# A ConvFFN in seven block products for eight: the whole down projection and five pairs of up tiles of one layer

## The chip, the cores and the metric

The kernel runs on one core of one Trainium2 chip. The metric is the device time of one execution, in microseconds (us). Before the change it is 1056.19 us, the median of three runs that lie between 1055.73 and 1057.11 us. The engines are named as the profile names them: PE (TensorE, the matrix engine; PEld is its weight load), DVE (VectorE), ACT (ScalarE), POOL (GpSimd) and SP (SyncE, which issues the transfers).

## The reference, cut to what matters

Two layers of an encoder work on 512 positions of 1024 channels, in float32. Each layer mixes the positions (a Fourier group and windowed attention, not touched here) and then runs a convolutional feed-forward block, the ConvFFN:

```python
def dwconv_centred(h, w, bias):
    hp = jnp.pad(h, ((0, 0), (1, 1), (0, 0)))
    return hp[:, :-2] * w[0] + hp[:, 1:-1] * w[1] + hp[:, 2:] * w[2] + bias

    # per layer l, with D_FF = 2816
        h = rmsnorm(x, norm2[l])
        up = dwconv_centred(h @ w_up[l], conv_w[l], conv_b[l])
        gate, val = up[..., :D_FF], up[..., D_FF:]
        x = x + (jax.nn.silu(gate) * val) @ w_down[l]
```

`w_up` has 1024 rows and 5632 columns, `w_down` 2816 rows and 1024 columns.

## The kernel before, in words

**Tiles.** Everything is kept transposed: a tile holds 128 channels on the partitions and the 512 positions along the free axis. `x[k]` (k = 0 to 7) is the residual, `h2[k]` the normed input of the ConvFFN. The columns of `w_up` are 44 row tiles of 128 channels here, 22 of the gate half and 22 of the value half; tile `fi` of the one is paired with tile `fi` of the other. I call such a pair a slot.

**Precision.** Every float32 operand of a matrix product is split into a high and a low part (`split`, `wsplit`): ACT copies the high part out (line 90), DVE subtracts it from the source for the low part (line 93). `mm3` then issues three matmuls for a product of two such operands: high by high (line 120), weight low by high (line 121), weight high by low (line 122). A weight tile of 512 columns therefore costs one ACT and one DVE instruction, `whi` and `wlo`, with five buffers each.

**The up projection (lines 705 to 730).** For each of the two tiles of a slot, 24 matmuls of 128x512 gather one product in one of six PSUM banks. DVE multiplies it with the row of reciprocal norms `rb2` into `u`; ACT makes `y = cw1*u + cb`; two `scalar_tensor_tensor` on DVE (`stt`, line 96) add the two neighbours. Then ACT takes the silu of the gate tile and the product of gate and value tile follows (line 728): on DVE in layer 0, on POOL in layer 1. The result is split again.

**The down projection (lines 740 to 758).** The 22 slots are done in two halves of eleven; after each half its eleven tiles are multiplied with `w_down`: for each of eight output tiles m, 33 matmuls of 128x512 into one bank, and DVE adds the bank to `x[m]`. In the last half the last m is done in two halves of 256 columns.

**What sets the order.** The program is recorded under a tile scheduler with a simulated timeline: it decides, when the program is built, in which order each engine's instructions stand. On the chip each engine then runs its own list in that order, and waits where an operand or a buffer is not there. Just ahead of the ConvFFN stands the second norm (`norm_tile`, then `col_rstd` with the matmuls of line 227, then `row_rstd` with those of line 234), which gives `rb2`; the products of the first slots need `h2` but not `rb2`, and so can stand among its instructions.

## Time and profile before

| what | value |
|---|---|
| median of three runs | 1056.19 us |
| the profiled execution, its own time | 1056.14 us |
| span of its trace | 1054.3 us |
| PE busy | 1038.2 us, 98% |
| DVE busy | 726.8 us, 69% |
| ACT busy | 507.9 us, 48% |
| POOL busy | 90.8 us, 9% |
| layer 1's ConvFFN | from about 716 us to the end at 1054.3 us |

The span is the time from the first to the last instruction of the trace; the profiled execution's own time is 1.84 us longer. A line of the trace is that of a helper where a helper issues the instruction: line 93 is every `tt` (tensor_tensor), line 96 every `stt`, line 90 every activation. So one goes by the names of the tiles: `tF<-ps,rb` is a product times `rb2`, `wlo<-wraw,whi` the low part of a weight, `x<-x,ps` the addition to the residual. A matmul's record is longer than its turn on PE, since matmuls are pipelined; what counts is the distance between the starts of two that follow each other.

### The profile page before, as it was taken

How to read it: one execution, taken by the hardware profiler on the slowest of the kernel's cores; microseconds unless marked ns; L12 is line 12 of the kernel's file. 1: busy time of each engine (PE TensorE's matmuls, PEld its weight loads, DVE VectorE, ACT ScalarE, POOL GpSimd, SP SyncE). 2: the span in 40 equal slices, each digit the busy share in tenths (PEclk: the TensorE clock that was granted, in tenths of full speed). 3: DMA queues.
4: the chain of work that ended last, by engine and by line, in shares of the span. 5: the costliest groups of instructions: out<-in, count | busy, mean ns of one | idle time of the engine just before them, and what ended most of it. 6: DMA issues, size and time to landing. Idle time of an engine off the chain costs nothing.

```text
span 1054.3 us, 14425 instructions
## 1 busy us (share of the span) xinstructions
PE 1038.2 (98%) x5107; PEld 873.2 (83%) x5107; DVE 726.8 (69%) x1384; ACT 507.9 (48%) x939; POOL 90.8 (9%) x164
## 2 busy tenths in 40 slices
PE   8998999999999999999999999999999999999998
PEld 8986778888888888888899887888888888888887
DVE  8878768697767777777519775478877336878632
ACT  5339755455444445455423785246554224454421
POOL 0004410000000000000000152001101000101100
PEclk9999999999999999999999999999999999999999
DMA  7232152332269833239856313333332333332241
GB/s 273 83 115 87 58 193 81 100 100 96 78 226 353 324 100 101 89 114 322 280 181 221 113 62 99 122 100 94 101 101 74 96 115 100 98 101 82 82 150 48
DMA packets 60475, 140.03 MB, mean 133 GB/s; under 512 B 6642, under 2 KB 22258, under 8 KB 60404
## 3 DMA queue, kind: packets, MB, share of 16 engines
q1 hardware_dynamic: 60404, 139.12, 40.5%
q8 instruction: 40, 0.66, 0.3%
q14 instruction: 31, 0.25, 0.1%
HBM read 116.02 MB, written 23.07 MB: 132 GB/s over the span
## 4 chain that ended last, share of the span: by engine, by line
PE 93%; DVE 2%; DMA 2%; ACT 1%; issue 1%; POOL 0%; SPq 0%; ACTq 0%; DVEq 0%; POOLq 0%
PE ps L122 28%; PE ps L120 28%; PE ps L121 28%; PE ps L118 3%; PE ps L548 2%; PE ps L541 2%; PE ps L529 1%; DMA wraw<-in_w_qkv_dram 1%; PE ps L234 1%; PE ps L227 1%; ACT tA L90 0%; DMA x<-in_xT_dram 0%; DVE tA L533 0%; ACT act L90 0%; PE ps L500 0%
## 5 line engine op out<-in xcount | busy, mean ns | idle before, releaser
L90 ACT ACTIVATE whi<-wraw 128x512 fp32r<-128x512 f32 (+1 forms) x296 | 182.0, 616 | 290.8 <-PE ps L122 278.4
L120 PE MATMUL ps<-act,whi 128*128 128x512 f32 x768 | 298.9, 390 | 0.0
L121 PE MATMUL ps<-act,wlo 128*128 128x512 f32 x768 | 298.3, 389 | 0.0
L122 PE MATMUL ps<-act,whi 128*128 128x512 f32 x768 | 298.2, 389 | 0.0
L93 DVE TENSOR_TENSOR wlo<-wraw,whi 128x512 fp32r<-128x512 f32 (+1 forms) x304 | 219.7, 726 | 103.4 <-ACT whi L90 102.0
L122 PEld LDWEIGHTS ps<-act,whi 128*128 128x128 f32 x768 | 144.2, 188 | 30.1
L120 PEld LDWEIGHTS ps<-act,whi 128*128 128x128 f32 x768 | 144.2, 188 | 29.7
L121 PEld LDWEIGHTS ps<-act,wlo 128*128 128x128 f32 x768 | 144.2, 188 | 29.7
L96 DVE SCALAR_TENSOR_TENSOR tF<-tF,pb,tF 128x511 f32<-128x511 f32 x176 | 133.5, 763 | 11.1 <-ACT tF L90 8.7
L93 DVE TENSOR_TENSOR tF<-ps,rb 128x512 f32<-128x512 f32 x104 | 71.2, 689 | 77.9 <-PE ps L122 64.7
L120 PE MATMUL ps<-slab,whi 128*128 128x512 f32 (+2 forms) x212 | 82.2, 388 | 0.0
L122 PE MATMUL ps<-slab,whi 128*128 128x512 f32 (+2 forms) x212 | 79.9, 380 | 0.4 <-DVE slab L93 0.3
L121 PE MATMUL ps<-slab,wlo 128*128 128x512 f32 (+2 forms) x212 | 80.0, 378 | 0.0
L90 ACT ACTIVATE tF<-tF,pb 128x512 f32<-128x512 f32 x88 | 71.7, 816 | 11.3 <-DVE tF L93 4.6
L93 DVE TENSOR_TENSOR x<-x,ps 128x512 f32<-128x512 f32 (+1 forms) x49 | 32.9, 674 | 36.5 <-PE ps L122 36.3
L93 POOL TENSOR_TENSOR tF<-tF,tF 128x512 f32<-128x512 f32 x22 | 30.2, 1371 | 256.1 <-DVE tF L96 224.1
L120 PE MATMUL ps<-pT,whi 128*128 128x512 f32 (+1 forms) x132 | 50.5, 383 | 0.0
L121 PE MATMUL ps<-pT,wlo 128*128 128x512 f32 (+1 forms) x132 | 50.5, 383 | 0.0
L122 PE MATMUL ps<-pT,whi 128*128 128x512 f32 (+1 forms) x132 | 50.5, 383 | 0.0
L538 POOL TENSOR_SCALAR tA<-tA,den 128x256 f32<-128x256 f32 (+1 forms) x64 | 37.4, 590 | 145.1 <-DVE den L537 144.6
L533 DVE CUSTOM_DVE_ANT_0 tA<-ps,pb,nsink 128x256 f32<-128x256 f32 (+1 forms) x64 | 37.8, 603 | 14.5 <-PE ps L529 9.7
L122 PEld LDWEIGHTS ps<-slab,whi 128*128 128x128 f32 x212 | 39.7, 188 | 8.3 <-DVE slab L93 0.9
(178 smaller groups left out, 1485.0 us busy)
## 6 DMA issues: line engine op xcount, KB each, us to landing
wraw<-in_w_up_dram SPq DMA_DIRECT2D x88, 512.0 KB, 3.5
wraw<-in_w_down_dram SPq DMA_DIRECT2D x32, 512.0 KB, 3.7
kept<-tA SPq DMA_DIRECT2D x56, 256.0 KB, 5.7
whi<-kept SPq DMA_DIRECT2D x28, 256.0 KB, 3.0
wlo<-kept SPq DMA_DIRECT2D x28, 256.0 KB, 3.0
kept<-tA SPq DMA_DIRECT2D x32, 192.0 KB, 4.4
wraw<-in_w_down_dram SPq DMA_DIRECT2D x32, 192.0 KB, 2.4
wraw<-in_w_o_dram SPq DMA_DIRECT2D x8, 512.0 KB, 3.7
```

Source lines behind the costliest of these rows:

```text
L90: return nc.scalar.activation(out, in_, func, **kw)
L93: return (eng or nc.vector).tensor_tensor(out, a, b, op=op)
L96: return nc.vector.scalar_tensor_tensor(out=out, in0=a, scalar=s, in1=b, op0=op0, op1=op1)
L118: nc.tensor.matmul(out, a[0], b[0], start=start, stop=stop, **kw)
L120: nc.tensor.matmul(out, a[0], b[0], start=start, stop=False, **kw)
L121: nc.tensor.matmul(out, a[1], b[0], start=False, stop=False, **kw)
L122: nc.tensor.matmul(out, a[0], b[1], start=False, stop=stop, **kw)
L227: nc.tensor.matmul(pt[:, 2 * b:2 * b + 2], acc[:, b * P:(b + 1) * P], ones2, start=True, stop=True)
L533: nc.vector.tensor_tensor_reduce(out=pr[:, :n], in0=sc[:, :n], in1=mask[:, m0:m0 + n], scale=qs_scale[p][:, i, e:e + 1], scalar=nsink[:, l ...
L538: nc.gpsimd.tensor_scalar(pr[:, :n], pr[:, :n], den[:, i:i + 1], 1.0, op0=ALU.mult, op1=ALU.mult)
L541: tr = nc.tensor.transpose(pp[:, j * P:(j + 1) * P], pr[:, j * P:(j + 1) * P], ident)
L548: pv = nc.tensor.matmul(py[64 * e:64 * e + 64, i0 * P:(i1 + 1) * P], vp[:, j, 64 * g:64 * g + 64], pT[:, half, e, b0:b0 + 2 * (i1 - i0) + ...
```

## The change

Layer 0 is unchanged. Layer 1's ConvFFN becomes a function of its own, `conv_ffn_seven`. It uses the Winograd form of Strassen's product: two 2x2 block matrices are multiplied with seven block products for eight, and with sums of blocks instead. In the form used here the blocks of the weight give four sums s1 to s4, those of the moving operand four sums T1 to T4, and the positions are cut in two halves of 256 columns.

- **Slots.** The 22 slots are done in three groups of 6, 8 and 8 (`GROUPS`), each followed by its part of the down projection. All eight PSUM banks are used in turn (`BANKS8`), the two "tp" banks too, which `col_rstd` and `row_rstd` also use.
- **Up.** In 17 of the slots `up_eight` does what was done before. In slots 4, 8, 11, 16 and 19 (`SEVEN`) `up_seven` makes both tiles of the pair together: 84 matmuls of 128x256 in three banks X, Y and Z, in place of 48 of 128x512. It sums weights on DVE (four of 512 columns), splits seven weight blocks for four, and puts the two `u` together from the banks.
- **Sums of h2.** `seven_h` makes T1 to T4 of `h2` in the first four slots, into buffers that earlier parts of the program have left.
- **Gate.** The product of gate and value tile is a `tt` on DVE, no longer on POOL.
- **Sums of the gated tiles.** `seven_gu` takes two gated tiles, makes T1 to T4 of them and splits all seven blocks.
- **Down.** For each pair of output rows seven products, each of kp k-tiles (3 in the first group, 4 in the others) by three matmuls of 128x256, and after each an addition of 256 columns to `x` on DVE. For the first three pairs of rows the sum s1 is made by the transfers: a load issued by SP and a second one issued by POOL that adds to it (`accum_op`). The other sums are DVE's.

The helpers move down by four lines: `tt` is line 97 in the changed kernel, `stt` line 100, `act` line 94, `mm3` lines 124 to 126, `col_rstd` and `row_rstd` lines 231 and 238.

```diff
+GROUPS = [(0, 6), (6, 8), (14, 8)]
+SEVEN = (4, 8, 11, 16, 19)
+BANKS8 = ("mm", "mm", "mm", "av", "sc", "sc", "tp", "tp")
...
+    def sums_of_b(b1, b2):
+        t13, t24 = temp(512, "tF"), temp(512, "tF")
+        tt(t13[:, LO], b1[:, HI], b1[:, LO], ALU.subtract)
+        tt(t13[:, HI], b2[:, HI], b1[:, HI], ALU.subtract)
+        tt(t24[:, LO], t13[:, LO], b2[:, HI], ALU.subtract)
+        tt(t24[:, HI], t24[:, LO], b2[:, LO], ALU.add)
+        return t13, t24
+
+    def parts(g, src, keys, room):
+        two = [next(room), next(room)]
+        split(*two, src)
...
+    def seven_h(k, l, h2, room):
+        b = [temp(512, "tF") for _ in range(2)]
+        for i in range(2):
+            act(b[i], x[k + 4 * i], scale=g2[:, l, k + 4 * i:k + 4 * i + 1])
...
+        t13, t24 = sums_of_b(*b)
+        parts(g, t13, ("T1", "T3"), room)
+        parts(g, t24, ("T2", "T4"), room)
+        return g
+
+    def seven_gu(b1, b2, room):
+        t13, t24 = sums_of_b(b1, b2)
+        one = next(room)
+        g = dict(B11=[one[:, LO], one[:, HI]])
+        split(*g["B11"], b1[:, LO])
+        parts(g, b2, ("B21", "B22"), room)
+        parts(g, t13, ("T1", "T3"), room)
+        parts(g, t24, ("T2", "T4"), room)
+        return g
...
+    def up_seven(l, fi, h2, ts, rb2):
+        a, b = [wload(t["w_up"][l, fi + z * FT], 1024) for z in range(2)]
+        a11, a12, a21, a22 = a[:, :512], a[:, 512:], b[:, :512], b[:, 512:]
+        X, Y, Z = [third()[:, LO] for _ in range(3)]
...
+        product(X, wsplit(a11), "B11", True)
+        act(ua[:, LO], X)
+        s1, s2, s3, s4 = [temp(512, "tA") for _ in range(4)]
+        tt(s1, a21, a22, ALU.add)
+        product(Y, wsplit(s1), "T1", True)
+        act(ub[:, HI], Y)
+        product(Z, wsplit(a12), "B21", True)
+        tt(ua[:, LO], ua[:, LO], Z, ALU.add)
+        tt(s3, a11, a21, ALU.subtract)
+        tt(s2, s3, a22, ALU.subtract)
+        product(X, wsplit(s2), "T2")
...
+        product(X, wsplit(a22), "T4")
+        tt(ub[:, LO], X, rb2[:, LO], ALU.mult)
+        tt(ub[:, HI], ub[:, HI], rb2[:, HI], ALU.mult)
+        yield ub
...
+    def first_two(l, mp, f0, kp):
+        n = kp * P
+        s1 = temp(n, "tA")
+        nc.sync.dma_start(s1, wd(l, 2 * mp + 1, f0, kp, 0))
+        nc.gpsimd.dma_start(s1, wd(l, 2 * mp + 1, f0, kp, 1), accum_op=ALU.add)
...
+    def conv_ffn_seven(l, h2, rb2):
+        room, ts = h_rooms(), []
+        for f0, nf in GROUPS:
+            kp = nf // 2
...
+                us = (up_seven if f0 + n in SEVEN else up_eight)(l, fi, h2, ts, rb2)
...
+                if len(ts) < 4:
+                    ts.append(seven_h(len(ts), l, h2, room))
+                gate(ys)
...
+                else:
+                    gu.append(seven_gu(upper, ys[0], groom))
...
+            for mp in range(3):
+                products(mp, first_two(l, mp, f0, kp) if mp else ready)
+            for mp in range(KT // 2):
+                products(mp, other_five(l, mp, f0, kp, mp == 3))
...
+        if l == L - 1:
+            conv_ffn_seven(l, h2, rb2)
+            break
```

Three places show how this moves instructions.

**PE, at the second norm of layer 1.** The products `ps_1576`, `ps_1584`, `ps_1593` and `ps_1601` are the first four of the up projection before the change, `ps_1575`, `ps_1607` and `ps_1583` those after it; `acc` is the sum of squares of the norm. Before:

```order
L122 MATMUL ps_1576_7036<-act_1563_7003,whi_1574_7032 128x512
L122 MATMUL ps_1584_7077<-act_1563_7003,whi_1582_7073 128x512
L122 MATMUL ps_1593_7123<-act_1559_6981,whi_1591_7119 128x512
L120 MATMUL ps_1593_7123<-act_1563_7003,whi_1591_7119 128x512
L121 MATMUL ps_1593_7123<-act_1563_7003,wlo_1592_7120 128x512
L122 MATMUL ps_1593_7123<-act_1563_7003,whi_1591_7119 128x512
L121 MATMUL ps_1601_7164<-act_1527_6847,wlo_1598_7157 128x512
L122 MATMUL ps_1601_7164<-act_1527_6847,whi_1597_7156 128x512
L227 MATMUL ps_1565_7009<-ones2_118,acc_1517_6802 128x2 x4
```

After:

```order
L124 MATMUL ps_1561_6987<-act_1486_6636,whi_1555_6961 128x512
L125 MATMUL ps_1561_6987<-act_1486_6636,wlo_1556_6962 128x512
L126 MATMUL ps_1561_6987<-act_1486_6636,whi_1555_6961 128x512
L124 MATMUL ps_1575_7035<-act_1524_6827,whi_1571_7027 128x512
L125 MATMUL ps_1575_7035<-act_1524_6827,wlo_1572_7028 128x512
...
L125 MATMUL ps_1575_7035<-act_1563_7003,wlo_1574_7032 128x512
L126 MATMUL ps_1575_7035<-act_1563_7003,whi_1573_7031 128x512
L231 MATMUL ps_1565_7009<-ones2_118,acc_1517_6802 128x2 x4
L124 MATMUL ps_1607_7178<-act_1524_6827,whi_1603_7170 128x512
```

Between the last product of the mixer's output (`ps_1561`) and the matmuls of `col_rstd` there stood 78 matmuls of four up products; now there stand the 24 of one.

**DVE, among the up slots.** Before, in the middle of a half (`tF<-ps` is `u`):

```order
L93 TENSOR_TENSOR wlo_1939_8954<-wraw_1937_8951,whi_1938_8953 128x512
L96 SCALAR_TENSOR_TENSOR tF_1920_8861<-tF_1919_8859,pb_96,tF_1920_8861 128x511 x2
L93 TENSOR_TENSOR wlo_1941_8958<-wraw_1937_8951,whi_1940_8957 128x512
L93 TENSOR_TENSOR tF_1927_8900<-ps_1926_8875,rb_1569_7023 128x512
L93 TENSOR_TENSOR wlo_1948_9000<-wraw_1946_8997,whi_1947_8999 128x512
L96 SCALAR_TENSOR_TENSOR tF_1928_8902<-tF_1927_8900,pb_96,tF_1928_8902 128x511 x2
```

After, around the fourth slot (`tF_1654<-tF_1654,tF_1662` is the gate, `tF_1665`, `tF_1666` and `sq` belong to `seven_h`, `tF_1671`, `tF_1672` and `pT` to `seven_gu`):

```order
L97 TENSOR_TENSOR tF_1654_7385<-tF_1654_7385,tF_1662_7426 128x512
L97 TENSOR_TENSOR tF_1666_7435<-tF_1665_7434,tF_1664_7431 128x256
L97 TENSOR_TENSOR tF_1671_7450<-tF_1631_7284 128x256
L97 TENSOR_TENSOR tF_1671_7450<-tF_1654_7385,tF_1631_7284 128x256
L97 TENSOR_TENSOR sq_1668_7441<-tF_1665_7434,room_1667_7440 128x512
L97 TENSOR_TENSOR tF_1666_7435<-tF_1666_7435,tF_1664_7431 128x256
L97 TENSOR_TENSOR pT_1673_7458<-tF_1654_7385,pT_1673_7458 128x512
L97 TENSOR_TENSOR tF_1672_7451<-tF_1671_7450,tF_1654_7385 128x256
L97 TENSOR_TENSOR pT_1673_7458<-tF_1671_7450,pT_1673_7458 128x512
L97 TENSOR_TENSOR tF_1680_7473<-tF_1680_7473,ps_1679_7472 128x256
L97 TENSOR_TENSOR room_1670_7445<-tF_1666_7435,sq_1669_7444 128x512
```

Weight splits stood between every two of the other instructions; now eleven instructions in a row split no weight.

**DVE, where a group of slots ends and its down projection begins.** Before, in the down projection of the second half:

```order
L93 TENSOR_TENSOR wlo_2069_9659<-wraw_2067_9656,whi_2068_9658 128x512
L93 TENSOR_TENSOR x4_78<-x4_78,ps_2057_9568 128x512
L93 TENSOR_TENSOR wlo_2071_9663<-wraw_2067_9656,whi_2070_9662 128x512
L93 TENSOR_TENSOR wlo_2074_9669<-wraw_2072_9666,whi_2073_9668 128x384
L93 TENSOR_TENSOR wlo_2078_9711<-wraw_2076_9708,whi_2077_9710 128x512
L93 TENSOR_TENSOR x5_79<-x5_79,ps_2066_9620 128x512
```

After, at the end of the first group (`tF_1709<-tF_1709,tF_1723` is the last gate, `m4` a split T block of the last pair of gated tiles):

```order
L97 TENSOR_TENSOR x0_74<-x0_74,ps_1728_7728 128x256
L97 TENSOR_TENSOR x2_76<-x2_76,ps_1733_7757 128x256
L97 TENSOR_TENSOR x4_78<-x4_78,ps_1741_7792 128x256
L97 TENSOR_TENSOR tF_1709_7651<-tF_1709_7651,tF_1723_7706 128x512
L97 TENSOR_TENSOR wlo_1743_7804<-tA_1737_7783,whi_1742_7803 128x384
L97 TENSOR_TENSOR wlo_1751_7830<-tA_1747_7824,whi_1750_7829 128x384
L97 TENSOR_TENSOR wlo_1753_7844<-wraw_1746_7819,whi_1752_7843 128x384
L97 TENSOR_TENSOR tF_1724_7712<-tF_1709_7651,tF_1698_7586 128x256
L97 TENSOR_TENSOR tF_1725_7713<-tF_1724_7712,tF_1709_7651 128x256
L97 TENSOR_TENSOR tA_1765_7909<-wraw_1762_7902,tA_1763_7907 128x384
L97 TENSOR_TENSOR pT_1674_7463<-tF_1709_7651,pT_1674_7463 128x512
L97 TENSOR_TENSOR tA_1780_7991<-wraw_1777_7984 128x384
```

One addition to `x` came per output tile, with four weight splits; now additions of 256 columns, weight sums, the gate and the sums of the last gated pair stand together.

More of the change, by code (lines that the diff above doesn't have):

```diff
@@ new lines, in parts, with h_rooms @@
+    def parts(g, src, keys, room):
+        two = [next(room), next(room)]
+        split(*two, src)
+        for key, cols in zip(keys, (LO, HI)):
+            g[key] = [z[:, cols] for z in two]
+    def h_rooms():
+        for tag in ("th0", "th1", "tl0", "tl1", "wt0", "wt1", "v", "accA", "accF"):
+            yield cp.tile([P, 512], F32R, tag=tag, name=nm("room"), bufs=1)
+        z = sp.tile([P, 1024], F32R, tag="ropetab", name=nm("room"), bufs=1)
+        yield from (z[:, :512], z[:, 512:])
+        for _ in range(2):
+            yield tp.tile([P, 516], F32R, tag="tail", name=nm("room"), bufs=2)[:, :512]
+        for _ in range(2):
+            yield temp(512, "sq", F32R)
+        yield cp.tile([P, 512], F32R, tag="room", name=nm("room"), bufs=1)
@@ new lines, in seven_gu, with up_eight @@
+    def seven_gu(b1, b2, room):
[7 more added lines that the diff above has]
+        return g
+    def up_eight(l, fi, h2, ts, rb2):
+        for z in range(2):
+            w = wchunks(t["w_up"][l, fi + z * FT], 1024)
+            o = third()
+            for k in range(KT):
+                mm3(o, [q[:, (k % 4) * P:(k % 4 + 1) * P] for q in w[k // 4]], [h2[k][:, s, :] for s in range(2)],
+                    k == 0, k == KT - 1)
+            u = temp(512, "tF")
+            tt(u, o, rb2, ALU.mult)
+            yield u
@@ new lines, in conv, with gate, wd @@
+    def conv(l, m, u):
+        y = temp(512, "tF")
+        act(y, u, AF.Identity, scale=cw[:, l, 1, m:m + 1], bias=cb[:, l, m:m + 1])
+        stt(y[:, 1:], u[:, :-1], cw[:, l, 0, m:m + 1], y[:, 1:], ALU.mult, ALU.add)
+        stt(y[:, :-1], u[:, 1:], cw[:, l, 2, m:m + 1], y[:, :-1], ALU.mult, ALU.add)
+        return y
+    def gate(ys):
+        act(ys[0], ys[0], AF.Silu)
+        tt(ys[0], ys[0], ys[1], ALU.mult)
+    def wd(l, m, f0, kp, half):
+        return t["w_down"][l, m, :, (f0 + half * kp) * P:(f0 + (half + 1) * kp) * P]
@@ new lines, in other_five @@
+    def other_five(l, mp, f0, kp, first):
+        n = kp * P
+        left, right = wtile(), wtile()
+        for i in range(2):
+            nc.sync.dma_start(left[:, i * n:(i + 1) * n], wd(l, 2 * mp + i, f0, kp, 0))
+        for i in (1, 0):
+            nc.sync.dma_start(right[:, i * n:(i + 1) * n], wd(l, 2 * mp + i, f0, kp, 1))
+        a11, a21, a12, a22 = left[:, :n], left[:, n:2 * n], right[:, :n], right[:, n:2 * n]
+        if first:
+            yield "X", wsplit(a11), "B11", 0, 0, False
+            s1 = temp(n, "tA")
+            tt(s1, a21, a22, ALU.add)
+            yield "Y", wsplit(s1), "T1", 1, 1, False
+        s2, s3, s4 = [temp(n, "tA") for _ in range(3)]
+        tt(s3, a11, a21, ALU.subtract)
+        tt(s2, s3, a22, ALU.subtract)
+        yield "X", wsplit(s2), "T2", 0, 1, False
+        yield "Z", wsplit(a12), "B21", 0, 0, True
+        yield "X", wsplit(s3), "T3", 1, 1, True
+        tt(s4, a12, s2, ALU.add)
+        yield "Y", wsplit(s4), "B22", 0, 1, True
+        yield "X", wsplit(a22), "T4", 1, 0, True
```

59 lines of the change are left out of this document (56 added, 3 removed).

## The prediction

> **What bounds the kernel now.** I read the page's shares first, then the chain of waits, then the busy time by stage.
>
> ```profile
> span 1054.3 us, 14425 instructions
> PE 1038.2 (98%) x5107; PEld 873.2 (83%) x5107; DVE 726.8 (69%) x1384; ACT 507.9 (48%) x939; POOL 90.8 (9%) x164
> PE 93%; DVE 2%; DMA 2%; ACT 1%; issue 1%; POOL 0%; SPq 0%; ACTq 0%; DVEq 0%; POOLq 0%
> ```
>
> PE carries 93% of the chain, so the count of its columns sets the time, as long as nothing else holds it. Four stretches of layer 1's ConvFFN (columns: window, length, then busy time and instruction count of PE, PEld, DVE, ACT, POOL; clock; DMA share; GB/s) show how far the others are from that:
>
> ```profile
> 718.00:880.00 162.00, 162.00 (x716) 134.15 (x715) 106.91 (x147) 69.85 (x108) 15.58 (x11) 1.00 0.31 98
> 880.00:943.00 63.00, 63.00 (x279) 52.18 (x278) 49.43 (x63) 31.44 (x47) 7.73 (x6) 1.00 0.30 93
> 943.00:1000.00 57.00, 57.00 (x253) 47.19 (x252) 41.85 (x56) 26.37 (x40) 6.85 (x5) 1.00 0.30 94
> 1000.00:1054.00 54.00, 51.06 (x257) 43.45 (x255) 16.38 (x26) 10.12 (x17) 0.00 (x0) 0.99 0.31 97
> ```
>
> PE has no idle time before the tail and runs at clock 1.00; DVE is busy 66% of the first stretch and 78% of the second. This is the room into which the change puts its sums.
>
> **Prices.** PE's are the distances of starts, at 512 columns and in the last product, which is done at 256:
>
> ```profile
> 721.57 0.39 PE L121 MATMUL ps<-act,wlo 128*128 128x512 f32 x1
> 721.80 0.39 PE L122 MATMUL ps<-act,whi 128*128 128x512 f32 x1
> 722.02 0.39 PE L120 MATMUL ps<-act,whi 128*128 128x512 f32 x1
> 722.25 0.39 PE L121 MATMUL ps<-act,wlo 128*128 128x512 f32 x1
> ...
> 1049.46 0.28 PE L120 MATMUL ps<-pT,whi 128*128 128x256 f32 x1
> ...
> 1050.66 0.28 PE L121 MATMUL ps<-m,wlo 128*128 128x256 f32 x1
> 1050.78 0.28 PE L122 MATMUL ps<-m,whi 128*128 128x256 f32 x1
> ```
>
> 0.68/3 = 0.227 us and 1.32/11 = 0.120 us: a matmul of half the columns costs 53%, not 50%. DVE's prices, the same way:
>
> ```profile
> 717.00 0.68 DVE L93 TENSOR_TENSOR wlo<-wraw,whi 128x512 fp32r<-128x512 f32 x1
> 717.60 0.68 DVE L93 TENSOR_TENSOR tF<-ps,rb 128x512 f32<-128x512 f32 x1
> 718.20 3.39 DVE L96 SCALAR_TENSOR_TENSOR tF<-tF,pb,tF 128x511 f32<-128x511 f32 x5
> 721.50 0.69 DVE L93 TENSOR_TENSOR wlo<-wraw,whi 128x512 fp32r<-128x512 f32 x1
> ...
> 303.85 1.03 DVE L93 TENSOR_TENSOR tA<-m,tA 128x384 fp32r<-128x384 f32 x2 [2.09 <-ACT tA L90]
> 305.27 0.56 DVE L93 TENSOR_TENSOR tA<-m,tA 128x384 fp32r<-128x384 f32 x1 [0.40 <-ACT tA L90]
> ...
> 575.27 0.75 DVE L93 TENSOR_TENSOR act<-pT,ropetab 128x256 f32<-128x256 f32 x2
> 575.94 0.68 DVE L93 TENSOR_TENSOR slab<-tF,slab 128x512 fp32r<-128x512 f32 x1
> ```
>
> A tt of 512 columns takes 0.60 us (717.00 to 717.60), an stt 3.30/5 = 0.66, a tt of 384 columns 1.03 - 0.56 = 0.47, one of 256 columns 0.67/2 = 0.335. Here too a half costs more than half.
>
> **What PE saves.** Down: before 8 x 2 products, of which the last is halved: 495 matmuls at 0.2267 and 66 at 0.120, 120.1 us. After: 22 slots make 11 pairs of k tiles, by four pairs of rows 44 blocks of 21 matmuls at 0.120: 110.9 us. That is 9.3 us less. Up: a slot costs 48 x 0.2267 = 10.88 us, by `up_seven` 84 x 0.120 = 10.08; five of them save 4.0 us. Together **-13.3 us**. Seven for eight would be 12.5%; the dearer half columns leave 7.6%.
>
> **What DVE gets.** By these prices a slot of `up_eight` takes four wlo (2.40), two u (1.20), four stt (2.64) and now the gate (0.60), 6.85 us, beside 10.88 us of PE; half of a `seven_gu` (5 x 0.335 + 3 x 0.60 = 3.48 for two slots) makes it 8.6. A slot of `up_seven` takes seven wlo and four sums of 512 columns (6.6), the u parts (2.3), the neighbours (2.64), the gate and half a `seven_gu`: 13.9 us beside 10.08 of PE. In the first four slots each `seven_h` adds 4 x 0.335 + 2 x 0.60 = 2.54. A pair of rows of the down projection takes 8.4 us beside 10.08 (four k tiles) or 7.05 beside 7.56 (three). Over the whole ConvFFN that is 322 us of DVE beside 346 of PE, 93%; by the same prices it is 187 before.
>
> The gate costs DVE something already when it runs on POOL:
>
> ```profile
> 727.18 0.74 DVE L96 SCALAR_TENSOR_TENSOR tF<-tF,pb,tF 128x511 f32<-128x511 f32 x1
> 728.06 1.30 POOL L93 TENSOR_TENSOR tF<-tF,tF 128x512 f32<-128x512 f32 x1 [4.42 <-DVE tF L96]
> 728.44 1.47 DVE L96 SCALAR_TENSOR_TENSOR tF<-tF,pb,tF 128x511 f32<-128x511 f32 x1
> ```
>
> A DVE instruction beside it is held 0.73 us longer than its like, so the move itself is worth 0.1 us a slot to DVE. It is the sums that load it.
>
> **Where DVE makes PE wait.** An average of 93% would do if the work came evenly. It doesn't, and DVE runs its list in order. So I take, from the order of the changed program, each stretch that begins where DVE waits for a product of PE and ends where PE waits for DVE's result, count what stands between on both engines, and price it. Where DVE's sum is longer, PE stands still for the difference.
>
> 1. The second norm. In the trace before, DVE runs without a gap into the last `acc`:
>
> ```profile
> 699.13 0.75 DVE L96 SCALAR_TENSOR_TENSOR act<-x,pa,act 128x512 fp32r<-128x512 f32 x1
> 701.45 0.69 DVE L93 TENSOR_TENSOR acc<-acc,sq 128x512 f32<-128x512 f32 x1
> 707.24 0.95 PE L227 MATMUL ps<-ones,acc 128*128 128x2 f32 x8
> 689.60:707.20 17.60, 17.60 (x79) 14.60 (x78) 12.87 (x22) 7.95 (x14) 0.00 (x0) 1.00 0.32 89
> ```
>
> The 78 up matmuls between the mixer's last product and L227 kept PE busy for 17.6 us. The 24 that now stand there are 5.4 us, to about 695; the last `acc` is due at 702.1 less the two wlo that have left DVE's list, 700.9. That gives 6; by counts (25 tt and 8 stt, 20.3 us, beside 16.3 of PE) 4. I take **5**. None of it was there before: L227 came 5 us after `acc`.
> 2. The first `up_seven`. From the second up product's u to the last split of `seven_h`, which T2 and T4 wait for: 39 tt and 14 stt, 23 tt of 256 columns, 40.4 us; PE has 132 matmuls of 512 and 35 of 256, 34.1. **6.8**, with 0.5 for the wlo behind it.
> 3. The first group's end. From the T4 product of slot 4 to the first addition to `x[0]`: 7 tt of 512, 11 of 384, 14 of 256 and 6 stt, 18.0 us; PE 11 matmuls of 512 and 75 of 256, 11.5. **6.5**. Behind the late addition stand those of `x[2]` and `x[4]`, whose banks the next products need.
> 4. The second group's end. From slot 11's T4: 31 tt of 512, 18 of 256 and 10 stt, 31.3 us; PE 61 and 99 matmuls, 25.7. **5.6**, and 1.2 at slot 11 itself.
> 5. The third group's end, in the same way from slot 19: 30.7 beside 25.5, **5.2**, and 1.2.
>
> Sum: 5 + 6.8 + 6.5 + 6.8 + 6.4 = 31.5 us. In each, PE's later instructions wait behind the one that waits. By the same count the ConvFFN before has no such stretch, as the 63.00 of 63.00 us of PE show.
>
> **What else is added.** ACT gets 104 instructions, on an engine at 43 to 50% of the stretches above: nothing. The nine accumulating transfers are of a kind that this trace lacks. The nearest row:
>
> ```profile
> wraw<-in_w_down_dram SPq DMA_DIRECT2D x32, 512.0 KB, 3.7
> ```
>
> Below, nothing, as the loads are issued ahead of the stall; above, one such time in each group, 3 x 3.7 = 11 us. I take nothing, since POOL, rid of 22 gates, has little else to issue between. [...] The weight is reloaded for each matmul as before:
>
> ```profile
> L122 PEld LDWEIGHTS ps<-act,whi 128*128 128x128 f32 x768 | 144.2, 188 | 30.1
> ```
>
> A load takes 188 ns by its record, more than the 120 ns between the half matmuls of the tail, which each have one of their own; so there it is overlapped.
>
> The tail stays:
>
> ```profile
> 1051.09 0.42 DVE L93 TENSOR_TENSOR x<-x,ps 128x256 f32<-128x256 f32 x1 [3.53 <-PE ps L122]
> 1051.54 0.33 SPq L758 DMA_DIRECT2D out_dram<-x  x1
> ```
>
> The last addition and transfer are of 256 columns before and after.
>
> **The sum.** 1054.3 - 13.3 + 31.5 = 1072.5 us of span; with the 1.84 us that lie around the span of the profiled execution (1056.14, against a median of 1056.19) **1074 us**.
>
> **Rivals.**
>
> - *DVE's work is absorbed.* DVE has 7% less than PE on average, and PE stays the bound: 1056.1 - 13.3 = 1043 us. For it speaks the average; against it that instructions run in order, and that the surplus lies in five places with no slack behind. It decides by DVE's price: the five stretches hold some 141 us of DVE work, so at 12.6% less, 0.525 us for 512 columns instead of 0.60, stalls fall by 17.8 us to 13.7, about the gain. No row shows a tt of 512 columns below 0.60. 10%.
> - *Half the stalls.* Part of what I count as one after the other is hidden, by banks or by DVE having run ahead: 1056.1 - 13.3 + 16 = 1059 us. The order allows little of it. 8%.
> - *The accumulating transfers come late.* s1 is the second operand that each pair of rows needs; if its two transfers in series are not there, each group stands one landing more: 1074 + 11 = 1085 us. The loads before are ahead of need, which speaks against it. 7%.
> - *Weight loads show behind short matmuls.* If a load of 188 ns could not overlap, the 1344 half matmuls (924 down, 420 up) would each take 0.188 us more: +253 us, 1327 us. The tail's 0.120 us speaks against it, as those 66 matmuls would have needed 0.308 each. 2%. [...]
> - *The change does not do what it says.* If the scheduler had kept eight products, the time would stay at 1056; but the order shows 1344 matmuls of 128x256, so 1%.
>
> **Chances and range.** The forecast keeps 72%; within it the five stalls may be off by a quarter, 8 us, so 1066 to 1082. The range takes in the bounds of the entry and of the transfers and reaches to the half case: 1058 to 1085. Outside lie the first rival, the weight loads and tails of some 5%. What a measurement of this kernel can tell from no change is about 0.2%, 2 us. Faster holds the first rival and a little of the second, 12%; the same 3%, between them; slower 85%.
>
> **What would show it.** In the profile after: PE's busy time down to about 1025 us with 0.120 us between half matmuls everywhere, and 95 to 96% of the span; DVE's busy time up by 135, to about 860 us, with DVE as releaser of PE's idle time. PE idle in five places of 4 to 7 us: ahead of `col_rstd`, in the first `up_seven` at its T products, and at the start of each of the three down projections, there behind `x`, `wlo` and `m4` of DVE. DVE without a gap over each of these. POOL without the x22 group. Wrong would be: no gaps and a shorter span (the first rival), gaps released by a DMA on `tA` (the third), or half matmuls further apart than 0.120 us (the fourth). If the gaps are there but shorter, my prices of DVE are too high.

## The result and the profile after

The changed kernel takes **1097.22 us** (median of four runs, 1096.44 to 1098.41), the kernel before 1056.09 us in the same comparison: ratio **1.0389, 95% interval 1.0371 to 1.0407**. It is slower by 3.9%, where 1.7% was forecast; the time lies above the range's upper end of 1085 us.

From the page of the changed kernel, the span, the shares, the granted clock in 40 slices and the chain of waits by engine:

```profile
span 1095.1 us, 16049 instructions
PE 1052.7 (96%) x5650; PEld 904.3 (83%) x5650; DVE 835.6 (76%) x1693; ACT 556.8 (51%) x1043; POOL 69.6 (6%) x151
PEclk9999999999999999999999999898899998999989
PE 82%; DVE 10%; ACT 3%; issue 2%; DMA 2%; POOL 0%; SPq 0%; DVEq 0%; ACTq 0%; POOLq 0%
```

DVE stands in 10% of the chain now, for 2% before, and the row of the clock has a new kind of mark: eights, where the clock was not granted in full. PE's busy time has not gone down by 13 us but up by 14, though it has less to do. Stage by stage (window, length, busy times and counts of PE, PEld, DVE, ACT, POOL, then the granted clock):

```profile
690.00:710.00 20.00, 16.76 (x61) 12.42 (x61) 13.50 (x23) 7.58 (x13) 1.01 (x1) 0.74 0.17 52
745.00:766.00 21.00, 13.56 (x78) 12.38 (x78) 17.99 (x35) 12.79 (x24) 0.00 (x0) 0.76 0.17 43
766.00:778.00 12.00, 12.00 (x72) 10.61 (x71) 9.50 (x18) 5.34 (x9) 0.00 (x0) 1.00 0.33 100
778.00:798.00 20.00, 17.13 (x106) 15.26 (x105) 19.89 (x45) 9.68 (x19) 0.00 (x0) 0.83 0.25 79
798.00:838.00 40.00, 40.00 (x250) 36.19 (x249) 32.89 (x63) 18.75 (x32) 0.00 (x0) 1.00 0.35 116
872.00:880.00 8.00, 6.15 (x38) 5.20 (x38) 8.00 (x15) 5.44 (x10) 0.00 (x0) 1.00 0.23 71
905.00:930.00 25.00, 21.68 (x140) 19.42 (x140) 23.83 (x48) 10.43 (x19) 0.00 (x0) 0.86 0.28 85
930.00:976.00 46.00, 46.00 (x300) 42.21 (x299) 35.93 (x63) 20.43 (x32) 0.00 (x0) 1.00 0.33 103
1009.00:1020.00 11.00, 9.15 (x51) 7.96 (x50) 9.43 (x17) 6.55 (x14) 0.00 (x0) 0.84 0.34 81
1045.00:1066.00 21.00, 18.18 (x112) 16.25 (x111) 19.43 (x39) 9.31 (x16) 0.00 (x0) 0.84 0.34 104
```

The norm (690), the first `up_seven` (745) and the three group ends (778, 905, 1045) are the stages in which PE waits; they are the five of the prediction. Between them PE has idle time only at the four later `up_seven`, of which the rows at 872 and 1009 are two. In the five the clock is at 0.74 to 0.86; between them it is at 1.00, but for the last `up_seven` (0.84 in the row at 1009). PE's rows at the first `up_seven`, and some at full clock:

```profile
755.13 0.58 PE L124 MATMUL ps<-room,whi 128*128 128x256 f32 x1 [6.69 <-ACT room L94]
755.51 0.41 PE L125 MATMUL ps<-room,wlo 128*128 128x256 f32 x1
756.68 0.58 PE L126 MATMUL ps<-sq,whi 128*128 128x256 f32 x1 [0.75 <-DVE sq L97]
...
757.90 0.41 PE L124 MATMUL ps<-room,whi 128*128 128x256 f32 x1
758.12 0.41 PE L125 MATMUL ps<-room,wlo 128*128 128x256 f32 x1
...
820.61 0.28 PE L124 MATMUL ps<-slab,whi 128*128 128x256 f32 x1
820.72 0.28 PE L125 MATMUL ps<-slab,wlo 128*128 128x256 f32 x1
```

PE waits 6.69 and 0.75 us for the T blocks of `seven_h` (`room` and `sq`), and then runs at 0.213 us for a half matmul where it takes 0.12 otherwise. The first row names ACT, which copies the high part out; that copy had itself waited 1.07 us for a sum of DVE's. DVE was at work the whole time: in the 5 us from 750 on it is busy 4.86 us and PE has no instruction (first row, columns as in the stages above), and the last split that PE waits for here is DVE's row at 755.94:

```profile
750.00:755.00 5.00, 0.00 (x0) 0.00 (x0) 4.86 (x10) 3.29 (x6) 0.00 (x0) 0.64 0.25 79
...
755.94 0.69 DVE L97 TENSOR_TENSOR sq<-tF,room 128x512 fp32r<-128x512 f32 x1
```

The stretches of half clock, cut out exactly by the record of the granted clock:

```profile
696.73:706.97 10.24, 8.71 (x23) 6.29 (x24) 5.86 (x10) 2.63 (x5) 1.01 (x1) 0.50 0.18 51
751.35:761.58 10.23, 5.70 (x24) 5.27 (x25) 9.57 (x20) 6.13 (x11) 0.00 (x0) 0.50 0.06 22
782.06:788.89 6.83, 6.42 (x27) 5.55 (x26) 6.82 (x16) 2.88 (x6) 0.00 (x0) 0.50 0.01 2
911.77:918.59 6.82, 6.33 (x23) 5.28 (x24) 6.81 (x15) 3.13 (x6) 0.00 (x0) 0.50 0.01 3
1014.17:1017.58 3.41, 3.41 (x14) 3.12 (x14) 3.41 (x7) 1.76 (x4) 0.00 (x0) 0.50 0.47 144
1051.72:1058.55 6.83, 6.56 (x28) 5.93 (x28) 6.73 (x13) 2.60 (x5) 0.00 (x0) 0.50 0.11 18
```

Six stretches, 44.4 us together, each one, two or three times 3.41 us long, and each begins in or just behind a wait of PE. Their starts lie 54.6, 30.7, 129.7, 102.4 and 37.5 us apart, which is 16, 9, 38, 30 and 11 times 3.413 us: in this trace the clock changes only at the ends of windows of that length, which follow each other without a break. So the length of a wait alone does not decide. The third and the fifth `up_seven` have the same pair of waits, 0.9 and 1.4 us by the distances of starts (from 873.02 and 874.02 on; from 1011.02 and 1012.02 on). At the third a window ends between the two, at 874.23, and the clock stays up; at the fifth both lie in the window that ends at 1014.18, and the clock falls there.

**The account.** I took the distance of each two starts on PE and subtracted what the first of them costs at full clock (0.2267 or 0.120 us). What is left is charged as slow pace as far as the first matmul ran at half clock, and as waiting otherwise. Against my count of DVE's lateness, in us:

| place | counted | waited | slow pace |
|---|---|---|---|
| the norm | 5 | 4.5 | 3.8 |
| the first `up_seven` | 6.8 | 8.2 | 2.3 |
| first group's end | 6.5 | 5.2 | 2.4 |
| the second and third `up_seven` | 1.2 | 3.8 | 0 |
| second group's end | 5.6 | 6.1 | 2.3 |
| the fourth and fifth `up_seven` | 1.2 | 3.8 | 1.6 |
| third group's end | 5.2 | 5.3 | 2.5 |
| the last addition | 0 | 0.8 | 0 |
| sum with small rests | 31.5 | 37.8 | 15.1 |

So 1054.3 - 13.3 + 37.8 + 15.1 = 1093.9 us. The last 1.2 us are of the start of the program, which the change does not touch: between 20 and 40 us the clock is 0.91 in this execution and 1.00 in the profiled one of before. That makes the 1095.1 us of the span. The 13.3 us that PE was to save are there: no residue is left over. They are outweighed by two terms, one counted and one that the prediction did not have.

### The profile page after: what moved, and what is told of

It reads as the page before. It is cut to its first block, busy times and chain, and to the rows that moved or that the text cites. A ratio compares the mean times of both kernels' runs of the same rounds, so it can differ in the third digit from the quotient of the medians.

```text
span 1095.1 us, 16049 instructions
## 1 busy us (share of the span) xinstructions
PE 1052.7 (96%) x5650; PEld 904.3 (83%) x5650; DVE 835.6 (76%) x1693; ACT 556.8 (51%) x1043; POOL 69.6 (6%) x151
## 4 chain that ended last, share of the span: by engine, by line
PE 82%; DVE 10%; ACT 3%; issue 2%; DMA 2%; POOL 0%; SPq 0%; DVEq 0%; ACTq 0%; POOLq 0%
PE ps L124 24%; PE ps L126 24%; PE ps L125 24%; PE ps L122 3%; DVE tF L97 2%; DVE wlo L97 2%; PE ps L761 2%; DVE tF L100 2%; PE ps L754 1%; DMA wraw<-in_w_down_dram 1%; PE ps L742 1%; ACT whi L94 1%; DVE act L100 1%; DVE acc L97 1%; DVE tA L97 1%
## 5 line engine op out<-in xcount | busy, mean ns | idle before, releaser
L124 PE MATMUL ps<-act,whi 128*128 128x512 f32 (+1 forms) x748 | 287.5, 385 | 3.5 <-ACT whi L94 2.9
L126 PE MATMUL ps<-act,whi 128*128 128x512 f32 (+1 forms) x748 | 286.7, 384 | 1.9 <-DVE act L100 1.9
L125 PE MATMUL ps<-act,wlo 128*128 128x512 f32 (+1 forms) x748 | 286.8, 384 | 0.4 <-DVE wlo L97 0.4
L97 DVE TENSOR_TENSOR wlo<-wraw,whi 128x512 fp32r<-128x512 f32 (+1 forms) x287 | 190.7, 668 | 61.2 <-ACT whi L94 59.2
L97 DVE TENSOR_TENSOR tF<-ps,rb 128x512 f32<-128x512 f32 (+1 forms) x99 | 66.3, 674 | 51.5 <-PE ps L126 40.0
L97 DVE TENSOR_TENSOR x<-x,ps 128x256 f32<-128x256 f32 (+1 forms) x116 | 55.5, 491 | 28.8 <-PE ps L126 28.0
L94 ACT ACTIVATE whi<-tA 128x512 fp32r<-128x512 f32 (+1 forms) x68 | 40.5, 604 | 48.6 <-PE ps L126 47.2
L124 PE MATMUL ps<-pT,whi 128*128 128x256 f32 (+1 forms) x196 | 63.7, 326 | 1.3 <-ACT pT L94 1.3
L125 PE MATMUL ps<-pT,wlo 128*128 128x256 f32 (+1 forms) x196 | 63.6, 325 | 0.0
L126 PE MATMUL ps<-pT,whi 128*128 128x256 f32 (+1 forms) x172 | 56.6, 331 | 0.0
L124 PEld LDWEIGHTS ps<-slab,whi 128*128 128x128 f32 x240 | 45.1, 192 | 13.4 <-ACT whi L94 6.4
L125 PEld LDWEIGHTS ps<-slab,wlo 128*128 128x128 f32 x240 | 46.5, 194 | 6.4 <-DVE wlo L97 2.0
L126 PEld LDWEIGHTS ps<-slab,whi 128*128 128x128 f32 x240 | 46.4, 194 | 5.9 <-DVE slab L97 0.9
```

What stands on the lines that cost most here:

```text
L94: return nc.scalar.activation(out, in_, func, **kw)
L97: return (eng or nc.vector).tensor_tensor(out, a, b, op=op)
L124: nc.tensor.matmul(out, a[0], b[0], start=start, stop=False, **kw)
L125: nc.tensor.matmul(out, a[1], b[0], start=False, stop=False, **kw)
L126: nc.tensor.matmul(out, a[0], b[1], start=False, stop=stop, **kw)
```

## The experiments

The theory after the result (A): DVE's work comes in heaps, PE waits for it, and an idle PE also loses half of its clock for a while. The rivals (B, with their meaning in each run): short matmuls, a fuller DVE or the parts of the change cost by themselves.

### Waits alone, in the kernel before

```diff
                     o = psum(FFN_BANKS[nps[0] % len(FFN_BANKS)])
+                    for _ in range({(4, 0): 3, (8, 0): 7, (16, 0): 14}.get((fi, z), 0) if l else 0):
+                        tt(h2[0][:, 1, :], f(h2[0][:, 1, :]), f(h2[0][:, 1, :]), ALU.max)
```

> The kernel before, with nothing of the change, in which DVE rewrites the low part of h2[0] with itself (same values) 3, 7 and 14 times ahead of three up products of layer 1 (slots 4, 8 and 16). The products behind wait for it, so PE stands still, by the count of DVE instructions, for about 1.1, 3.7 and 8.5 us. Theory A (an idle PE loses its clock, and runs at half of it for a multiple of 3.41 us after): no half clock after the first, 3.4 to 6.8 us of it after the second, 6.8 to 10.2 us after the third, the span 1054.3 + 13.3 + 4 to 7 = 1071 to 1075 us. Theory B (the low clock comes from what the change adds, short matmuls or a fuller DVE): clock 1.00 throughout, span 1054.3 + 13.3 = 1067.6.

Measured: 1082.35 us, ratio 1.0238 (1.0221 to 1.0255); span 1081.0. Its three places, and the stretches between, by stage:

```profile
738.00:748.00 10.00, 7.25 (x24) 5.64 (x25) 6.59 (x10) 3.12 (x5) 2.72 (x2) 0.83 0.18 57
748.00:784.00 36.00, 36.00 (x160) 29.82 (x159) 28.22 (x39) 18.16 (x27) 4.15 (x3) 1.00 0.31 102
784.00:798.00 14.00, 10.52 (x34) 7.83 (x33) 7.84 (x13) 3.34 (x5) 1.57 (x1) 0.76 0.16 43
798.00:938.00 140.00, 140.00 (x620) 115.91 (x619) 83.00 (x116) 53.95 (x83) 9.71 (x7) 1.00 0.31 98
938.00:958.00 20.00, 10.01 (x31) 7.40 (x30) 12.95 (x19) 3.34 (x5) 1.55 (x1) 0.66 0.10 31
```

PE at the first and at the third place:

```profile
740.64 0.49 PE L121 MATMUL ps<-act,wlo 128*128 128x512 f32 x1 [2.76 <-DVE wlo L93]
741.25 0.80 PE L122 MATMUL ps<-act,whi 128*128 128x512 f32 x1
...
950.52 0.79 PE L122 MATMUL ps<-act,whi 128*128 128x512 f32 x1 [9.14 <-DVE act L93]
951.11 0.63 PE L120 MATMUL ps<-act,whi 128*128 128x512 f32 x1
951.53 0.63 PE L121 MATMUL ps<-act,wlo 128*128 128x512 f32 x1
```

Nothing of the change is in this kernel, no half matmul has been added and no sum, and the clock falls at each of the three waits and nowhere else in layer 1, to 0.43 us for a matmul of 512 columns. B falls. The half clock lasted 3.41, 6.83 and 13.66 us; the waits were longer than I had counted (18.1 us by the account above for 13.3, since DVE also had to catch up with the weight splits that stood behind its burst), and the slow pace added 7.0: 1054.3 + 18.1 + 7.0, and 1.2 at the program's start again, is 1080.6 of the 1081.0. One miss of the theory's sizes: I had expected no half clock behind the first wait, which was to be 1.1 us and was 2.76.

The lengths are one, two and four times 3.41 us, and the distances of the starts are multiples of it, as in the changed kernel. A single wait of 2.76 us was enough here, and at the second group's end of the changed kernel no row names a wait above 1.12 us and the clock fell all the same. What decides in these traces is how much of one window is idle. I laid the windows over all fourteen traces from 690 us on and took as idle what the distance of two starts has beyond 0.227 or 0.120 us. Of the windows at full clock, 41 hold 2.02 us of idle time or more, and half clock follows each of them; it follows none of the others, of which 62 hold 1.0 to 1.99 us. Behind a window at half clock another one follows where it holds 0.96 us or more, and none where it holds 0.76 or less.

### The norm's place alone

```diff
         room, ts = h_rooms(), []
+        nps[0] = 7
```

> The changed kernel, with the turn of the eight banks begun so that the first six up products are in banks other than the two that the norm uses; more of them then stand ahead of the norm's matmuls. Theory A (each late place costs its DVE backlog, and a half clock behind it): the 8.2 us at the norm go, but DVE has done none of its work earlier, so by count the first up_seven waits 4 us longer; about 1097 - 4 = 1093 us, one stretch of half clock less or the second one longer. Theory B (the places are independent): 1097 - 8 = 1089 us.

Measured: 1099.91 us, ratio 1.0407 (1.0392 to 1.0423), not faster than the changed kernel's 1.0389. Stage by stage:

```profile
690.00:710.00 20.00, 20.00 (x94) 16.72 (x93) 15.26 (x25) 9.05 (x15) 0.00 (x0) 1.00 0.22 80
745.00:766.00 21.00, 9.66 (x38) 8.37 (x39) 18.85 (x38) 13.03 (x23) 0.00 (x0) 0.54 0.03 9
```

The norm's wait and its half clock are gone, as A and B both said. At the first `up_seven` PE now loses 20.4 us by the distances of its starts, for 10.5. Neither time came, 1093 us of A or 1089 of B. A was right that the wait comes back, but it had 4 us where 9.9 came, and the half clock there lasts six windows of 3.41 us. PE reaches the T product that waits at 740.2 us, for 748.3 in the changed kernel; DVE's split that ends the last wait there (`sq`) starts at 757.77, for 755.94. DVE can begin on the slots only when the reciprocal norms are there (717.49 us, for 709.78), and from then on to the end of that split it is at work for 41 us, with no gap longer than 0.5. PE arriving earlier only waits longer. The norm's late place was in truth a part of the wait for the four `seven_h`.

### Each half of the change alone

Down projection only:

```diff
-SEVEN = (4, 8, 11, 16, 19)
+SEVEN = ()
...
-                if len(ts) < 4:
+                if SEVEN and len(ts) < 4:
```

> The changed kernel with no up_seven and no seven_h (all 22 slots by up_eight), the down projection in seven products. Theory A: gain 9.3 us; the norm costs its 8.2 as it stands; the three group ends have by count 3.5, 2.1 and 2.1 us of DVE backlog, with one window of half clock each at most (1.7): 1056 - 9.3 + 8.2 + 7.7 + 2 to 5 = 1065 to 1068 us. Theory B (the seven products of the down projection are themselves what costs most): near 1080 us and above, group ends as in the changed kernel (8 us each).

Measured: 1070.38 us, ratio 1.0129 (1.0114 to 1.0144); span 1067.2. By the account: saved 9.3 by my sum, waited 17.7, slow pace 4.4, so 1054.3 - 9.3 + 22.1 = 1067.1. A's 1065 to 1068 us is missed by 2 us, B's 1080 by 10. The group ends lose 5.7, 3.0 and 3.0 us in place of 7.6, 8.4 and 7.8, without half clock.

Up projection only, with the down projection of the kernel before (eight products, halves of eleven slots):

```diff
-        for f0, nf in GROUPS:
+        for f0, nf in HALVES:
...
-                    gu.append(seven_gu(upper, ys[0], groom))
+                split(a[:, 0, :], a[:, 1, :], ys[0])
+                gu.append(a)
...
-            for mp in range(3):
-                products(mp, first_two(l, mp, f0, kp) if mp else ready)
-            for mp in range(KT // 2):
-                products(mp, other_five(l, mp, f0, kp, mp == 3))
+            for m in range(KT):
...
```

> The changed kernel's up projection (five up_seven, seven_h, gate on DVE, eight banks) with the down projection in eight products and two halves as before. Theory A: gain 4.0 us; the norm 8.2; the first up_seven 4.1 us of backlog by count and 1.7 to 3.4 of half clock; nothing at the ends of the halves: 1056 - 4 + 8.2 + 5.8 to 7.5 = 1066 to 1068 us. Theory B (the up_seven slots cost by themselves): PE idle in each of the five, 1075 us and above.

Measured: 1067.43 us, ratio 1.0104 (1.0089 to 1.0119); span 1065.4. By the account: saved 4.0, waited 9.2, slow pace 5.9: 1065.4. All of the loss is in two places, the norm (9.6 us) and the first `up_seven` (5.6); the other four `up_seven` cost nothing there.

Both halves alone lose 1.3 and 1.0%; together they lose 3.9, more than their sum, though the norm's loss is in both and should count once. What DVE is late with does not just add: at the group ends it costs 7.6 to 8.4 us with both halves and 3.0 to 5.7 with one.

### Keeping PE busy through two of the waits

```diff
+    zw = cp.tile([P, P], F32R, tag="zw", name="zw")
+    act(zw, zero[:, :P])
...
+                if fi + z == 0 and k > 3:
+                    for _ in range(5):
+                        nc.tensor.matmul(o, zw, h2[k - 2][:, 0, :], start=False, stop=False)
...
+                if fi == 2 and key == "T1" and k == 3:
+                    for i in range(54):
+                        nc.tensor.matmul(o, zw, ts[i % 3]["B11"][0], start=False, stop=False, skip_group_check=True)
```

> The changed kernel with matmuls of zero weights, which add zeros to a bank whose sum is open and wait for nothing, put in front of two of the waits: 20 of 512 columns (4.5 us) ahead of the norm's matmuls, 54 of 256 (6.5 us) ahead of the last T1 block of the first up_seven. They take PE time that was idle. Theory A (idle time, not the change's instructions, lowers the clock): no half clock at these two places; DVE's results come when they did, so only the slow matmuls behind them are won, some 3 us each: 1097 - 6 = 1091 us, with four stretches of half clock for six. Theory B (the clock falls with what DVE or the short matmuls do): half clock as before, and the time 1097 us or above, by up to 11 us where the fillers come on top.

Measured: 1095.99 us, ratio 1.0365 (1.0343 to 1.0387), by the intervals no different from the changed kernel's. The two stages:

```profile
690.00:710.00 20.00, 19.35 (x92) 15.49 (x91) 15.03 (x25) 8.97 (x14) 1.01 (x1) 1.00 0.22 61
745.00:766.00 21.00, 19.57 (x137) 17.71 (x136) 20.03 (x39) 13.00 (x24) 0.00 (x0) 1.00 0.17 50
```

The clock stays at 1.00 at both places: it is idleness that lowers it. But the 6 us did not come, nor A's 1091. At the two places 4.1 us were won (18.9 us of waiting and slow pace became 11.0 of fillers and 3.8 of waiting); behind them the first group's end lost 0.9 us more, the third `up_seven` 1.6 with a new stretch of half clock (its two waits now lie in one window), the third group's end 0.9. My reading is that DVE catches up while PE runs slowly, and that what it owes is asked for later; that the new stretch is nothing but the other phase of the windows is as likely for its 1.6 us. Either way the 15.1 us of slow pace are where the time went in the account, and not what would be won if the clock stayed up.

### The other parts of the change

The gate back on POOL:

```diff
-        tt(ys[0], ys[0], ys[1], ALU.mult)
+        tt(ys[0], ys[0], ys[1], ALU.mult, nc.gpsimd)
```

> The changed kernel with the product of gate and value tile on POOL, as before the change. Theory A (an instruction of DVE beside POOL's is held 0.73 to 0.83 us, so nothing is won by sparing it 0.60): 22 x 0.13 to 0.23 us more of DVE's time, half of it at the late places: 1097 to 1100 us. Rival (POOL takes the gate's 13 us off DVE): the late places lose 5.6 us by count and some half clock: 1088 to 1091 us.

Measured: 1103.78 us, ratio 1.0435 (1.0404 to 1.0467), with the runs further apart than elsewhere (1098.9 to 1107.5). Sparing DVE 22 instructions does not make the kernel faster; the rival's 1088 to 1091 is far off, and A's 1097 to 1100 is too low by 4. Why the runs lie apart was not traced. POOL's group is this:

```profile
L97 POOL TENSOR_TENSOR tF<-tF,tF 128x512 f32<-128x512 f32 x22 | 33.6, 1526 | 247.0 <-DVE tF L100 211.6 <-ACT tF L94 21.2 <-ACT whi L94 14.0
```

Each takes 1.53 us, for 1.37 in the kernel before. There the DVE instruction beside POOL's was held, 1.47 us for 0.74, and sixteen other ones, all `wlo`, take 1.74 for 0.68. That DVE and POOL hold each other is my reading of these rows; what makes them do so was not shown.

The nine sums s1 by DVE, without the accumulating transfers:

```diff
-        nc.gpsimd.dma_start(s1, wd(l, 2 * mp + 1, f0, kp, 1), accum_op=ALU.add)
+        s1b = temp(n, "tA")
+        nc.sync.dma_start(s1b, wd(l, 2 * mp + 1, f0, kp, 1))
+        tt(s1, s1, s1b, ALU.add)
```

> The changed kernel with the nine sums s1 of the down projection made by DVE from two plain loads, with no accumulating transfer. Theory A (transfers are in time, DVE is what is late): nine more additions on DVE, which by count lengthen the waits by 7 us, most of it ahead of the second and third group's ends: 1104 us, or up to 1108 with another window of half clock. Rival (the accumulating transfers hold the group ends): 1097 us or less.

Measured: 1108.04 us, ratio 1.0479 (1.0462 to 1.0497): waited 45.9 us for 37.8, slow pace 17.2, the upper end of A's 1104 to 1108. Nine more instructions of DVE, 5 us of work, cost the kernel about 10. The accumulating transfers were a help and not late: no wait of PE in the changed kernel from 680 us on names a transfer. In the changed kernel, the two transfers of an s1 (line, engine, count, size, median us from issue to landing):

```profile
tA<-in_w_down_dram SPq DMA_DIRECT2D x6, 256.0 KB, 3.8
tA<-in_w_down_dram POOLq DMA_DIRECT2D x6, 256.0 KB, 4.6
```

### Putting PE's work where DVE is behind

Down projection only, with the bank order of the second run:

```diff
-SEVEN = (4, 8, 11, 16, 19)
+SEVEN = ()
...
         room, ts = h_rooms(), []
+        nps[0] = 7
```

> The down projection alone (as in the run of that) with the bank order of the run on banks. With no seven_h in the first four slots DVE has time to spare there, so theory A expects the norm's 9.4 us to go here without coming back later, where with up_seven they came back larger; the first group's end 5.6 us by count, the others 2 each, one window of half clock or two: span 1054.3 - 9.3 + 10 + 0 to 3 = 1055 to 1058 us, 1057 to 1060 us. Theory B (the bank order is bad for the up slots in itself): 1070 us and above.

Measured: 1062.3 us, ratio 1.0047 (1.0033 to 1.0061); span 1061.6, a little above A's 1055 to 1058, since the group ends lost 6.1, 4.8 and 3.0 us for the counted 10 in all, and the start of the program 1.2. The norm's loss is gone and does not come back, as there is no `seven_h` behind it.

Then the first slot of the next group recorded ahead of each down projection (`slot` holds the body of the loop over the slots, down to the gate):

```diff
+        early = []
+        def slot(f0, nf, n):
...
+            return ys[0]
...
             for n in range(nf):
+                ys = early.pop() if early else slot(f0, nf, n)
...
+            if f0 + nf < FT:
+                early.append(slot(*GROUPS[GROUPS.index((f0, nf)) + 1], 0))
+            ready = list(first_two(l, 0, f0, kp))
             banks = [{} for _ in range(KT // 2)]
```

> The run before, with the first slot of the next group recorded ahead of each down projection, so that PE has 10.9 us of up products for which DVE must do 6.9 us, at the place where DVE is behind. Theory A (only the place of DVE's work costs): by count the first two group ends fall to 0.6 us in all, the last keeps 2.1 and 0.3: span 1054.3 - 9.3 + 3 = 1048 us, with one window of half clock 1050; 1050 to 1052 us, faster than the kernel before by 0.4 to 0.6%. Theory B (the short matmuls or DVE's load as such cost): no faster than the run before.

Measured: **1054.44 us, ratio 0.9974 (0.9965 to 0.9983)** against the kernel before. It beats both kernels. Its shares, and its three group ends by stage, the first two of which hardly wait (1.5 and 0.4 us):

```profile
PE 1032.6 (98%) x5470; PEld 884.8 (84%) x5470; DVE 799.7 (76%) x1614; ACT 532.9 (51%) x997; POOL 69.7 (7%) x151
...
775.00:790.00 15.00, 14.03 (x115) 13.62 (x114) 15.00 (x36) 6.90 (x14) 0.00 (x0) 1.00 0.25 79
790.00:1010.00 220.00, 219.87 (x1191) 191.50 (x1191) 186.51 (x325) 108.38 (x175) 5.25 (x6) 1.00 0.41 124
1010.00:1022.00 12.00, 10.67 (x77) 9.38 (x76) 11.82 (x25) 5.82 (x10) 0.00 (x0) 1.00 0.24 79
```

The clock stays at 1.00 through the ConvFFN, up to its last microsecond; DVE has as much to do as in the run before, only elsewhere beside PE's work. The span of 1052.7 us is 1054.3 - 9.3 + 5.7 of waits + 0.2 of slow pace + 1.2 at the start, and 0.6 that the account does not place. A had 1050 to 1052 us; it counted 3 us of waits and measured 5.7.

Groups of 8, 8 and 6 slots in the same version:

```diff
-GROUPS = [(0, 6), (6, 8), (14, 8)]
+GROUPS = [(0, 8), (8, 8), (16, 6)]
```

> The version with the next group's first slot ahead of the down projection, all slots by up_eight, with groups of 8, 8 and 6 slots for 6, 8 and 8. Theory A: by count no wait at the first two group ends, 3.2 us at the last and 0.3 at the end, as against 0.6, 2.1 and 0.3: the same time within 1 us, 1053 to 1056 us. Rival (the order of group sizes matters by itself): a difference of 3 us or more.

Measured: 1056.11 us, ratio 0.9990 (0.9981 to 0.9999). The waits went to the last group's end (5.9 us there, with a stretch of half clock). It is 1.7 us slower than the version before it, more than A's 1 and less than the rival's 3, and the two intervals just touch.

Two `up_seven` put back, in slots 12 and 17:

```diff
-SEVEN = ()
+SEVEN = (12, 17)
...
-            if SEVEN and len(ts) < 4:
+            if SEVEN and len(ts) < 4 and f0 + n >= 1 and (f0 + n) % 2:
```

> The version with the next group's first slot ahead of the down projection, to which two up_seven come back (slots 12 and 17, far from the group ends) and seven_h, spread over every second slot. Theory A (DVE's surplus shows wherever it is put): PE's work 1.6 us less, but by count 16 us of waits for 3, at the first group's end, at slot 12 and at the second group's end: 1054.3 - 10.9 + 16 + 2 to 6 = 1061 to 1065 us of span, 1063 to 1067 us. Rival (only the crowding of the first slots and the group ends cost): below the version without them, 1050 to 1053 us.

Measured: 1068.04 us, ratio 1.0101 (1.0086 to 1.0116); span 1065.3, with 16.9 us of waits and 5.4 of slow pace. One of its four sets of T blocks, that of slot 7, is made from x behind the first group's additions, so it leaves out the right values there, at the same work. A's 1063 to 1067 us is missed by 1 us. The next run is the same with all of `seven_h` in the first group:

```diff
-            if SEVEN and len(ts) < 4 and f0 + n >= 1 and (f0 + n) % 2:
+            if f0 + n in (1, 2, 4, 5):
```

> As the version with the next group's first slot ahead and two up_seven (slots 12 and 17), with seven_h in slots 1, 2, 4 and 5, so that the T blocks are made before x changes (in the run before this one, half of them were made from an x that the first group had already added to, so it left out the right T values, at the same amount of work). Theory A (DVE's surplus shows wherever it is put): by count 12 us of waits at the first group's end, 5.7 at the second's, 2.4 at the last: 1054.3 - 10.9 + 20 + 4 to 7 = 1067 to 1070 us of span, 1069 to 1072 us. Rival (only the crowding of the first four slots cost): as the version without up_seven, near 1054 us.

Measured: 1072.9 us, ratio 1.0148 (1.0134 to 1.0162); span 1071.0, with 21.0 us of waits for the counted 20, and 5.3 of slow pace. Two `up_seven` save PE 1.6 us and cost 16 and 20 us of waits and slow pace (22.3 and 26.3 us for the 5.9 without them): what `seven_h` and the weight sums add on DVE shows at the next group's end in both places that were tried. Neither place brought a gain, so five pairs of up tiles are work that DVE has no room for here.

## Why the prediction was wrong, point by point

- **What bounds the kernel; what PE saves; the direction: right.** At full clock half matmuls follow each other at 0.120 us, weights and all, and PE's own work fell by the 13.3 us of the sum. The rival on weight loads is out. The kernel is slower, as forecast, but by more than twice as much. PE's busy time was to fall to 1025 us and rose to 1052.7, since matmuls at half clock are busy for longer (0.41 us by the record of a half matmul, for 0.28).
- **DVE's prices: right; its load: 24 us too high.** The changed kernel's DVE is busy 835.6 us for the forecast 860. Most of the 24 us is a misreading of POOL's gate: I took one held instruction, 0.73 us longer than its like, and valued the move of the gate at 0.1 us a slot. In the kernel before, 20 instructions of DVE beside it take 1.47 us or more, some 20 us above their like in all, and in the changed kernel none does (`wlo<-wraw,whi` 668 ns on average for 726). So the move was worth some 0.3 us a slot.
- **The five places: right in place, a little small in sum.** 31.5 us were counted and 37.8 waited. The norm, the group ends and the first `up_seven` are within 1.5 us each. The step "1.2 at slot 11 itself" and its like for the third group were too small: the four later `up_seven` wait 7.6 us together, for 2.4. PE's rows at the second and third of them name ACT as what it waited for, the high part of a weight tile and a copy of a sum out of its bank; the prediction had put ACT's part at nothing. That this is all of the difference was not tried, and ACT's instructions alone do not make it: in the run of the up projection alone, PE waits nowhere at these four slots:

```profile
840.70 0.50 PE L124 MATMUL ps<-act,whi 128*128 128x512 f32 x1 [0.72 <-ACT whi L94]
841.42 0.50 PE L125 MATMUL ps<-act,wlo 128*128 128x512 f32 x1 [0.23 <-DVE wlo L97]
...
874.02 0.50 PE L124 MATMUL ps<-act,whi 128*128 128x512 f32 x1 [0.72 <-ACT whi L94]
875.65 0.38 PE L124 MATMUL ps<-room,whi 128*128 128x256 f32 x1 [1.13 <-ACT tF L94]
```

- **"PE stands still for the difference": this step failed.** I priced a wait as idle time and nothing else, and gave all that follows the full clock, because the rows of the stages before showed 1.00. They showed it because PE never waits there. The waits brought 44.4 us of half clock, of which 15.1 us are charged to slow matmuls; this is most of the 23 us between the forecast and the measured time (15.1 + 6.3 of longer waits + 1.2 at the start = 22.6). That idleness alone does it is shown by the kernel before with three waits added, and by the fillers, with which the clock stayed up. The fillers also show that the two terms are not independent: with the clock held up at two places the kernel did not get faster. So the 31.5 us were too little for what DVE's lateness costs in all, 52.9 us, and how these divide between waiting and slow pace depends on the run.
- **The rivals.** *DVE's work is absorbed* is out, as no row of DVE was cheaper. *Half the stalls* is out: 37.8 us were waited, not 16. *The accumulating transfers come late* is out: without them the kernel is slower still. The true alternative, a wait that also costs the clock behind it, was not among them; with the 15 us measured later it would have put the forecast near 1074 + 15 = 1089 us.
- **The entry as a cost of its own: only half right.** Its 5 us were measured as 4.5, but with it taken away the kernel did not gain: DVE's debt was asked for at the first `up_seven`. My five places are not independent where no slack of DVE lies between them; the sum of a way through all of them is one number, not five.
- **What stays open.** How much of the 15.1 us of slow pace would be lost as waiting if the clock never fell. With the fillers 4.1 of the 6.1 us at two places were won there, and 3.4 us came back further on, 1.6 of it with a new stretch of half clock; the other places were not tried. Why the four later `up_seven` wait 7.6 us beside the seven products of the down projection, and not without them, is open too.
